# The experts' last 32 slots on 512-wide column tiles, with their products at other places in an expert's order

## The chip, the cores and the metric

The kernel runs on one core of one Trainium2 chip. The metric is the device time of one execution in microseconds (us). The engines of a core are TensorE (PE; its weight loads, which overlap with its products, are listed as PEld), VectorE (DVE), ScalarE (ACT), GpSimd (POOL) and SyncE (SP, which here only issues DMAs).

## What is computed

One decoder layer on 2048 tokens of 1024 values: a mixer (gated linear attention beside dilated window attention), a mixture of experts, and a norm. The change touches the mixture of experts alone. Cut to that:

```python
def hier_moe(n, w_grp, b_grp, w_exp, b_exp, w1, w3, w2):      # n: 2048 x 1024
    g_idx = argmax(x @ w_grp + b_grp)                          # one of 4 groups
    top_v, top_i = top_k(e_logits of that group, 2)            # two of its 8 experts
    gate = softmax(top_v) * g_prob
    for each expert e, for its tokens xb:                      # 32 experts
        hb = silu(xb @ w1[e]) * (xb @ w3[e])                   # 1024 -> 512
        out[tokens] += gate * (hb @ w2[e])                     # 512 -> 1024
h = h + out;  y = rmsnorm(h)
```

All is float32, and each expert's weights are 6 MB.

## The kernel before

The layer runs in stages one after the other: the mixer (to about 1100 us of the span), router and table of tokens (to about 1310 us), the experts (to about 2165 us), and the final norm. Each expert has 160 slots for tokens in the table. The first 128 are one full tile. The last 32 are computed apart, on tiles of 32 columns of the array, so that four small products run side by side in its four column groups.

**Weights.** `weights(e)` loads an expert's six parts of 1 MB in the order w1 first half, w3 first half, w1 second half, w3 second half, w2 first half, w2 second half (SP, L1283) into six `raw` buffers, and splits each: `hi` is the rounded copy (ACT, L1288), `lo` the rest (DVE, L1288). `hi` and `lo` have five buffers each. The full tile is multiplied in three products (hi.hi, lo.hi, hi.lo) of rounded values; the last 32 slots multiply the raw float32 weights directly, and the trace shows each of these matmuls as two instructions.

**One expert e**, in the order of the code (L1416 to L1433):
- `up` (L1327): 48 products 128x512 of the token tile (`nh`, `nl`) with w1 and w3 (L1338 to L1340), first half of the weights, then second. Then the last 32 slots (L1347): four column groups, two for w1 and two for w3, each with 256 of the 512 columns and `nr` as the stationary operand, in tile `r`. Then h = silu(w1 part) * w3 part (ACT L1352, DVE L1353), and the same for the last slots, 64 partitions by 256 (hr, L1358, L1359).
- `across` (L1363): h is transposed on PE (L1365) and split into `hh` (ACT) and `hl` (DVE, L1368); hr is transposed (L1373) and copied to `ht` (DVE, L1375).
- `turn` (L1310): the next expert's token tile is transposed (L1313) and split (L1316). In one expert of four (e = 1, 5, 9, ...) `turn_last` does the same for the last slots of the next four experts, which gives `nr` (L1322, L1324).
- `down` (L1378): 24 products with w2 (L1387 to L1389), scaled by the gate (L1391 ACT, L1393 DVE) and added to the output in memory by an indirect DMA from POOL (L1394). Then the last slots' products (L1402): four column groups of 256 of the 1024 columns each, all 128 partitions scaled (L1405), added by a second indirect DMA (L1406).

After the last expert, blocks of finished tokens are gathered (L1235), normalized and written (L1250, L1252).

**What sets the order.** A planner in the compiler lays down a fixed order for every engine's queue. It plays the program through with times of its own; each engine takes, of the instructions that are ready in it, the one that stands first in the code. A later one gets in front only while earlier ones wait. `self.behind(later, earlier)` makes the planner put one instruction after another on an engine. On the chip an engine works its queue off strictly in that order, with semaphores for what comes from other engines.

Of the kernel before, what the change touches and what calls it, by code (L numbers as in the profile page):

```python
# [19 lines left out]
KD = D // 128  # L20
# [36 lines left out]
class Layer:  # L57
# [1113 lines left out]
    def moe(self):  # L1171
        tc, nc, a = self.tc, self.nc, self.a
        with self.moest as st:
# [9 lines left out]
            acc4 = self.acc.rearrange("t (g c) -> (t g) c", g=4)  # L1183
# [3 lines left out]
            i4A = keep.tile([128, NE], I32, name="i4")  # L1187
# [3 lines left out]
            def entries(es):  # L1191
# [10 lines left out]
                f4 = gp.tile([128, NE], F32, name="f4", bufs=1)  # L1202
                nc.vector.tensor_copy(f4[:, es], irA[:, es, 0])
                nc.vector.tensor_scalar(f4[:, es], f4[:, es], 4.0, self.gcol, OP.mult, OP.add)
                nc.vector.tensor_copy(i4A[:, es], f4[:, es])
# [104 lines left out]
            def turn(G):  # L1310
                tp = tps.tile([128, KD, 128], F32, name="tp")
                for k in range(KD):
                    nc.tensor.transpose(tp[:, k, :], G[:, k * 128:(k + 1) * 128], self.ident)  # L1313
# [13 lines left out]
            def up(w, x, nr=None):  # L1327
# [5 lines left out]
                for half in range(2):  # L1333
                    for m in range(2):
                        raw, hi, lo = w[m][half]
                        for kk in range(4):
                            k = half * 4 + kk
                            nc.tensor.matmul(ps[m], nh[:, k, :], hi[:, kk, :], start=k == 0, stop=False)  # L1338
                            nc.tensor.matmul(ps[m], nl[:, k, :], hi[:, kk, :], start=False, stop=False)  # L1339
                            nc.tensor.matmul(ps[m], nh[:, k, :], lo[:, kk, :], start=False, stop=k == KD - 1)  # L1340
                pr = None
                if nr is not None:
                    pr = rps.tile([128, 256], F32, name="r")
                    for k in range(KD):
                        for g in range(4):
                            raw = w[g // 2][k // 4][0]
                            nc.tensor.matmul(pr[32 * g:32 * g + 32], nr[:, k, :], raw[:, k % 4, (g % 2) * 256:(g % 2) * 256 + 256],  # L1347
                                             start=k == 0, stop=k == KD - 1, skip_group_check=True, tile_position=(0, 32 * g))
                h = gp.tile([128, 512], F32, name="h")
# [4 lines left out]
                hr = None  # L1354
                if nr is not None:
                    hr = gp.tile([128, 256], F32, name="hr")
                    by, to = (lambda t: t.rearrange("t (p k) -> t k p", k=2)), hr[64:128].rearrange("t (k p) -> t k p", k=2)
                    nc.scalar.activation(to, by(pr[0:64]), AF.Silu)  # L1358
                    nc.vector.tensor_tensor(to, by(pr[64:128]), to, OP.mult)  # L1359
                return h, hr  # L1360

            def across(h, hr):
                tp = mm.tile([128, 4, 128], F32, name="mm")  # L1363
# [189 lines left out]
```

## Time and profile before

| | us |
|---|---|
| median of 3 runs (2217.42 to 2219.65) | 2219.3 |
| the profiled execution | 2223.29 |
| its span, first to last instruction | 2221.3 |
| PE busy in it | 2086.3 |
| DVE busy | 1272.1 |
| ACT busy | 1060.2 |
| POOL busy | 474.5 |

Durations are taken from the profiled execution, which has 2.0 us around its span and lies 4.0 us above the median. Matmuls are pipelined: the next one starts before the last has ended, so the cost of one in a row of many is the distance between starts, not its own duration. A row of the timeline that stands for several instructions (x46) gives the start of the first and the time to the end of the last.

### The profile page before, as it was taken

Reading aid. Unit: us, or ns where it says so; the run is one execution under the profiler, and the core shown is the slowest. Engines: PE = TensorE matmul, PEld = TensorE weight load, DVE = VectorE, ACT = ScalarE, POOL = GpSimd, SP = SyncE. Lnnn points to the kernel's source line nnn. Section 1 sums busy time; section 2 is a strip of 40 time slices with the busy share of each in tenths; the row PEclk is TensorE's granted clock in tenths of the full one; section 3 lists DMA queues with packets and bytes.
Section 4 is the critical chain, followed back from the end, with each engine's and each line's share of the span. In section 5 each row is a group of like instructions: output and inputs, shape, how many; then the busy total and the mean of one; then the engine's idle time right before and its main releaser. Section 6 shows DMA issues by size and latency. Waiting matters only on the chain. (4 is left out here: it accounts for less than half of the span.)

```text
span 2221.3 us, 38624 instructions
## 1 busy us (share of the span) xinstructions
PE 2086.3 (94%) x15306; PEld 1567.7 (71%) x15306; DVE 1272.1 (57%) x2452; ACT 1060.2 (48%) x1809; POOL 474.5 (21%) x362
## 2 busy tenths in 40 slices
PE   7999999999997999999999968899999999999990
PEld 7799889799885766666667756567676766767760
DVE  5203336424435466666656766567767677777663
ACT  5412335523323366867723334355555555555552
POOL 2000000000002012351321342523212222222235
PEclk9999999999998999999999969999999999999995
DMA  8333333333316524453368728688888888878886
GB/s 254 109 124 100 114 124 110 102 113 124 109 68 190 178 68 138 146 135 100 88 204 279 238 80 293 198 290 305 298 294 281 307 308 304 305 279 287 307 277 234
DMA packets 189033, 436.59 MB, mean 197 GB/s; under 512 B 35041, under 2 KB 106530, under 8 KB 162978
## 3 DMA queue, kind: packets, MB, share of 16 engines
q1 hardware_dynamic: 139090, 347.65, 44.5%
q0 software_dynamic: 21488, 60.36, 10.4%
q10 hardware_dynamic: 28272, 26.09, 4.0%
q8 instruction: 122, 2.00, 0.4%
q14 instruction: 61, 0.50, 0.1%
HBM read 342.48 MB, written 92.08 MB: 196 GB/s over the span
## 5 line engine op out<-in xcount | busy, mean ns | idle before, releaser
L1288 DVE TENSOR_TENSOR lo<-raw,hi 128x2048 fp32r<-128x2048 f32 x192 | 438.8, 2289 | 121.8 <-ACT hi L1288 121.4
L1288 ACT CAST hi<-raw 128x2048 fp32r<-128x2048 f32 x192 | 365.1, 1906 | 198.5 <-DMA raw<-expert_w 181.0
L564 ACT ACTIVATE P<-P,st 128x256 f32<-128x256 f32 (+1 forms) x384 | 173.9, 455 | 96.8 <-DVE st L562 92.5
L213 PE MATMUL mm<-whi,nh 128*128 128x256 f32 x768 | 219.9, 286 | 0.0
L215 PE MATMUL mm<-whi,nl 128*128 128x256 f32 x768 | 218.1, 284 | 0.0
L214 PE MATMUL mm<-wlo,nh 128*128 128x256 f32 x768 | 217.7, 284 | 0.0
L1340 PE MATMUL mm<-lo,nh 128*128 128x512 f32 x512 | 207.3, 406 | 0.1
L1338 PE MATMUL mm<-hi,nh 128*128 128x512 f32 x512 | 204.6, 400 | 1.1 <-ACT nh L1316 1.1
L1339 PE MATMUL mm<-hi,nl 128*128 128x512 f32 x512 | 201.4, 393 | 0.0
L128 POOL TENSOR_TENSOR ss<-ss,mhalf 128x1 f32<-128x1 f32 (+3 forms) x40 | 34.6, 865 | 699.1 <-DVE ss L127 698.9
L562 DVE CUSTOM_DVE_ANT_0 P<-s,amask 128x256 f32<-128x256 f32 (+1 forms) x384 | 124.9, 362 | 66.2 <-PE s L558 42.6
L190 PE MATMUL mm<-nh,whi 128*128 128x512 f32 x384 | 154.5, 402 | 0.0
L191 PE MATMUL mm<-nl,whi 128*128 128x512 f32 x384 | 153.1, 399 | 0.0
L192 PE MATMUL mm<-nh,wlo 128*128 128x512 f32 x384 | 152.7, 398 | 0.0
L213 PEld LDWEIGHTS mm<-whi,nh 128*128 128x128 f32 x768 | 145.4, 189 | 2.0 <-issue 0.7
L214 PEld LDWEIGHTS mm<-wlo,nh 128*128 128x128 f32 x768 | 145.7, 190 | 0.8 <-DVE wlo L176 0.4
L215 PEld LDWEIGHTS mm<-whi,nl 128*128 128x128 f32 x768 | 144.9, 189 | 0.1
L1347 PE MATMUL r<-raw,nr 128*32 128x256 f32 x2048 | 143.0, 383 | 0.0
L1394 POOL DMA_INDIRECT acc<-y,it x32 | 93.9, 2934 | 228.7 <-ACT y L1391 222.5
L558 PE MATMUL s<-k,q 64*128 64x256 f32 (+1 forms) x768 | 132.8, 416 | 0.3 <-DVE st L562 0.3
L1340 PEld LDWEIGHTS mm<-lo,nh 128*128 128x128 f32 x512 | 96.7, 189 | 43.1 <-issue 19.4
L176 DVE TENSOR_TENSOR wlo<-raw,whi 128x1024 fp32r<-128x1024 f32 x48 | 57.0, 1221 | 112.7 <-ACT whi L175 112.7
(340 smaller groups left out, 4165.0 us busy)
## 6 DMA issues: line engine op xcount, KB each, us to landing
raw<-expert_w SPq DMA_DIRECT2D x192, 1024.0 KB
raw<-w_in ACTq DMA_DIRECT2D x48, 512.0 KB
fb<-fac SPq DMA_DIRECT2D x24, 384.0 KB
x<-x SPq DMA_DIRECT2D x16, 512.0 KB
og<-og SPq DMA_DIRECT2D x32, 256.0 KB
xr<-x SPq DMA_DIRECT2D x32, 256.0 KB
v<-av SPq DMA_DIRECT2D x8, 1024.0 KB
hp<-xr SPq DMA_DIRECT2D x32, 256.0 KB
```

The lines of the kernel that those rows point to most:

```text
L190: nc.tensor.matmul(ps, hi[:, k, ms], nh[q][:, k, :], start=k == 0, stop=False)
L191: nc.tensor.matmul(ps, hi[:, k, ms], nl[q][:, k, :], start=False, stop=False)
L192: nc.tensor.matmul(ps, lo[:, k, ms], nh[q][:, k, :], start=False, stop=k == KD - 1)
L213: nc.tensor.matmul(ps[:, j, :], h, hi[:, k, :], start=j == 0 and k == 0, stop=False, skip_group_check=True)
L214: nc.tensor.matmul(ps[:, j, :], h, lo[:, k, :], start=False, stop=False, skip_group_check=True)
L215: nc.tensor.matmul(ps[:, j, :], l, hi[:, k, :], start=False, stop=k == KD - 1, skip_group_check=True)
L564: nc.scalar.activation(P[:, h, 0:w], P[:, h, 0:w], AF.Exp, bias=nm, scale=-1.0, accum_out=dn)
L1288: split = nc.scalar.copy(hi, raw), nc.vector.tensor_tensor(lo, raw, hi.bitcast(F32), OP.subtract)
L1338: nc.tensor.matmul(ps[m], nh[:, k, :], hi[:, kk, :], start=k == 0, stop=False)
L1339: nc.tensor.matmul(ps[m], nl[:, k, :], hi[:, kk, :], start=False, stop=False)
L1340: nc.tensor.matmul(ps[m], nh[:, k, :], lo[:, kk, :], start=False, stop=k == KD - 1)
L1347: nc.tensor.matmul(pr[32 * g:32 * g + 32], nr[:, k, :], raw[:, k % 4, (g % 2) * 256:(g % 2) * 256 + 256], start=k == 0, stop=k == KD - 1, ...
```

## The change

The last 32 slots' products move and get twice the width; each becomes half as many instructions.
- `up_last` is new and is called ahead of `up`, except in expert 0. Its four column groups take two steps of the contraction at once: w1 and w3 for an even k, w1 and w3 for the odd one, 512 columns each. The two partial sums are added behind it (ACT copy, DVE add), then Silu, then two multiplies. `up`'s wide products are put behind `up_last`'s of the same half of the weights.
- `down_last` (with `across_last`, the transposes of hr) is new and is called ahead of `across`. Its four column groups are two steps of the contraction by two halves of 512 columns; ACT scales one half of the partitions, DVE scales the other and adds. The indirect add goes out in 64 rows of 512 values where it was 128 rows of 256. h's transposes are put behind its last product, and the next tile's transposes behind h's.
- h, hh, hl, hr and ht have one buffer each where it was two.
- Expert 0 turns expert 1's tile before `across`.

```diff
-            def turn(G):
+            def turn(G, after=None):
                 tp = tps.tile([128, KD, 128], F32, name="tp")
                 for k in range(KD):
...
+                    t = nc.tensor.transpose(tp[:, k, :], G[:, k * 128:(k + 1) * 128], self.ident)
+                    if after is not None:
+                        self.behind(t, after, "these cover the copies of the inner values")
                 nh = gp.tile([128, KD, 128], F32R, name="nh")
                 nl = gp.tile([128, KD, 128], F32R, name="nl")
                 self.turned = nc.scalar.copy(nh, tp), nc.vector.tensor_tensor(nl, tp, nh.bitcast(F32), OP.subtract)
...
                 nc.vector.tensor_copy(nr[:, :, 0:n], tp[:, :, 0:n])
                 return nr
-            def up(w, x, nr=None):
+            def up_last(w, nr):
+                pr = rps.tile([128, 512], F32, name="r")
+                halves = []
+                for k in range(0, KD, 2):
+                    for g in range(4):
+                        kk, raw = k + g // 2, w[g % 2][k // 4][0]
+                        lasts = nc.tensor.matmul(pr[32 * g:32 * g + 32], nr[:, kk, :], raw[:, kk % 4, :],
+                                                 start=k == 0, stop=k == KD - 2, skip_group_check=True, tile_position=(0, 32 * g))
+                    halves.append(lasts)
+                hr = gp.tile([128, 256], F32, name="hr", bufs=1)
+                sm = gp.tile([64, 512], F32, name="sm", bufs=1)
+                sg = gp.tile([64, 512], F32, name="sg", bufs=1)
+                nc.scalar.copy(sm, pr[64:128])
+                nc.vector.tensor_tensor(sm, pr[0:64], sm, OP.add)
+                nc.scalar.activation(sg[32:64], sm[0:32], AF.Silu)
+                by = lambda t, u: t[:, 256 * u:256 * u + 256].rearrange("t (p k) -> t k p", k=2)
+                for u in range(2):
+                    to = hr[64 + 32 * u:96 + 32 * u].rearrange("t (k p) -> t k p", k=2)
+                    nc.vector.tensor_tensor(to, by(sm[32:64], u), by(sg[32:64], u), OP.mult)
+                return hr, halves[1::2]
+            def up(w, x, halves=None):
                 nh, nl = x
                 ps = []
                 for m in range(2):
...
                         raw, hi, lo = w[m][half]
                         for kk in range(4):
                             k = half * 4 + kk
...
+                            first = nc.tensor.matmul(ps[m], nh[:, k, :], hi[:, kk, :], start=k == 0, stop=False)
+                            if halves and kk == 0:
+                                self.behind(first, halves[half], "the raw weights come free early")
                             nc.tensor.matmul(ps[m], nl[:, k, :], hi[:, kk, :], start=False, stop=False)
                             nc.tensor.matmul(ps[m], nh[:, k, :], lo[:, kk, :], start=False, stop=k == KD - 1)
...
+                h = gp.tile([128, 512], F32, name="h", bufs=1)
                 by, to = (lambda t: t.rearrange("t (a p k) -> t a k p", a=2, k=2)), (lambda t: t.rearrange("t (a k p) -> t a k p", a=2, k=2))
                 nc.scalar.activation(to(h), by(ps[0]), AF.Silu)
                 nc.vector.tensor_tensor(to(h), by(ps[1]), to(h), OP.mult)
...
-            def across(h, hr):
+                return h
+            def across(h, after=None):
                 tp = mm.tile([128, 4, 128], F32, name="mm")
                 for k in range(4):
...
+                    self.inner = nc.tensor.transpose(tp[:, k, :], h[:, k * 128:(k + 1) * 128], self.ident)
+                    if after is not None:
+                        self.behind(self.inner, after, "the last slots' products cover the inner values")
+                hh = gp.tile([128, 4, 128], F32R, name="hh", bufs=1)
+                hl = gp.tile([128, 4, 128], F32R, name="hl", bufs=1)
                 self.crossed = nc.scalar.copy(hh, tp), nc.vector.tensor_tensor(hl, tp, hh.bitcast(F32), OP.subtract)
...
-            def down(w2, x, it, irs, e=None):
...
+                return hh, hl
+            def across_last(hr):
+                tr = rps.tile([128, 2, 64], F32, name="r")
+                for c in range(2):
+                    nc.tensor.transpose(tr[:, c, :], hr[64:128, c * 128:(c + 1) * 128], self.ident[64:128, 64:128])
+                ht = gp.tile([128, 2, 2, 32], F32, name="ht", bufs=1)
+                nc.vector.tensor_copy(ht, tr.rearrange("p c (u s) -> p u c s", u=2))
+                return ht
+            def down_last(w2, hr, ir, i2, e):
+                ht = across_last(hr)
+                pr = rps.tile([128, 512], F32, name="r")
+                for k in range(0, 4, 2):
+                    raw = w2[k // 2][0]
+                    for g in range(4):
+                        kk, f = g // 2, g % 2
+                        last = nc.tensor.matmul(pr[32 * g:32 * g + 32], ht[:, k // 2, kk, :], raw[:, kk, f * 512:f * 512 + 512],
+                                                start=k == 0, stop=k == 2, skip_group_check=True, tile_position=(0, 32 * g))
+                yr = yp.tile([64, 512], F32, name="yr", bufs=2)
+                nc.scalar.activation(yr, pr[64:128], AF.Copy, scale=ir[64:128, 1:2].bitcast(F32))
+                nc.vector.scalar_tensor_tensor(yr, pr[0:64], ir[0:64, 1:2].bitcast(F32), yr, op0=OP.mult, op1=OP.add)
+                added(nc.gpsimd.indirect_dma_start(out=acc2, out_offset=bass.IndirectOffsetOnAxis(ap=i2, axis=0),
+                                                   in_=yr, in_offset=None, compute_op=OP.add), e)
+                return last
+            def down(w2, x, it, e=None):
+                hh, hl = x
                 y = yp.tile([128, D], F32, name="y", bufs=2)
                 gate = it[:, 1:2].bitcast(F32)
                 for f in range(2):
...
                         nc.vector.tensor_scalar(y[:, fs], py, gate, None, OP.mult)
                 added(nc.gpsimd.indirect_dma_start(out=self.acc, out_offset=bass.IndirectOffsetOnAxis(ap=it[:, 0:1], axis=0),
                                                    in_=y, in_offset=None, compute_op=OP.add), e)
...
-                h = across(*up((w1, w3), x, nr[:, :, at:at + 32]))
+                if e == 0:
+                    h = up((w1, w3), x)
+                hr, halves = up_last((w1, w3), nr[:, :, at:at + 32])
+                if e:
+                    h = up((w1, w3), x, halves)
                 at += 32
+                if e == 0:
+                    x = turn(G.pop(1))
+                    self.firstst.close()
+                    yp = pool("e_y", 1)
+                h = across(h, down_last(w2, hr, irA[:, e], i2A[:, e:e + 1], e))
                 if e + 1 < NE:
-                    x = turn(G.pop(e + 1))
+                    if e:
+                        x = turn(G.pop(e + 1), self.inner)
                     if e % 4 == 1:
                         nr, at = turn_last(R, 32 * min(4, NE - 1 - e)), 0
-                    for t, c in zip(self.turned, self.crossed):
+                    for t, c in zip(self.turned, self.crossed if e else ()):
                         self.behind(t, c, "what the tensor engine waits for comes first")
-                if e == 0:
-                    self.firstst.close()
-                    yp = pool("e_y", 1)
-                down(w2, h, itA[:, e], (irA[:, e], i4A[:, e:e + 1]), e)
+                down(w2, h, itA[:, e], e)
```

Left out of the diff: the index arithmetic (`i2 = 2 * token + group` for 64 partitions in place of `i4 = 4 * token + group` for 128) and the removed old lines of `up`, `across` and `down`, which the kernel above shows.

## Rows read from the trace of the kernel before

**Rows 1.** The page, busy time (share of the span) and instructions of each engine

```profile
PE 2086.3 (94%) x15306; PEld 1567.7 (71%) x15306; DVE 1272.1 (57%) x2452; ACT 1060.2 (48%) x1809; POOL 474.5 (21%) x362
```

**Rows 2.** Busy time by stretch: length, engines, granted clock, DMA share, GB/s

```profile
1420.60:1501.30 80.70, 79.69 (x557) 54.07 (x555) 57.60 (x46) 42.82 (x33) 21.87 (x10) 1.00 0.80 275
...
1603.60:1705.80 102.20, 102.20 (x737) 71.57 (x736) 71.92 (x54) 58.38 (x44) 24.08 (x13) 1.00 0.85 296
```

**Rows 3.** Waits, 1501 to 2155 us, SP and ACT: total, times, longest

```profile
SPq L1283 <- PE r L1347: 361.6, 46, 17.3
...
ACT hi L1288 <- DMA raw<-expert_w: 158.2, 140, 3.4
```

**Rows 4.** Order of time on PE, one expert: start, length, line, shapes, count

```profile
1653.80 0.50 PE L1338 MATMUL mm<-hi,nh 128*128 128x512 f32 x1
...
1657.20 1.05 PE L1347 MATMUL r<-raw,nr 128*32 128x256 f32 x10
1658.18 0.50 PE L1340 MATMUL mm<-lo,nh 128*128 128x512 f32 x1
...
1663.89 0.64 PE L1347 MATMUL r<-raw,nr 128*32 128x256 f32 x8
...
1666.96 2.79 PE L1347 MATMUL r<-raw,nr 128*32 128x256 f32 x46
1669.68 0.66 PE L1365 MATMUL mm<-ident,h 128*128 128x128 f32 x4
...
1671.14 0.33 PE L1373 MATMUL r<-ident,hr 64*128 64x64 f32 x2
1671.40 0.73 PE L1387 MATMUL mm<-hi,hh 128*128 128x512 f32 x2
...
1677.17 1.93 PE L1402 MATMUL r<-raw,ht 128*32 128x256 f32 x32
1679.04 0.50 PE L1338 MATMUL mm<-hi,nh 128*128 128x512 f32 x1
```

**Rows 5.** The same view, another expert

```profile
1615.96 3.22 PE L1347 MATMUL r<-raw,nr 128*32 128x256 f32 x54
```

**Rows 6.** Groups by line and shape: busy us, mean ns of one, idle before

```profile
L1347 PE MATMUL r<-raw,nr 128*32 128x256 f32 x1664 | 115.2, 383 | 0.0
...
L1353 DVE TENSOR_TENSOR h<-mm,h 128x512 f32<-128x512 f32 x26 | 18.0, 692 | 50.6 <-PE mm L1340 50.6
...
L1405 DVE TENSOR_SCALAR yr<-r,ir 128x256 f32<-128x256 f32 x25 | 11.9, 478 | 0.0
L1359 DVE TENSOR_TENSOR hr<-r,hr 64x256 f32<-64x256 f32 x26 | 11.1, 427 | 9.4 <-ACT hr L1358 9.1
...
L655 PE MATMUL mm<-f,ident 32*64 32x384 f32 x64 | 12.3, 495 | 0.0
```

**Rows 7.** Order of time on PE, an early expert, with the idle time before

```profile
1373.01 0.33 PE L1373 MATMUL r<-ident,hr 64*128 64x64 f32 x2
1373.78 1.93 PE L1402 MATMUL r<-raw,ht 128*32 128x256 f32 x30 [0.43 <-ACT hh L1368]
```

**Rows 8.** Order of time on DVE behind the wide products of rows 4

```profile
1667.13 0.69 DVE L1353 TENSOR_TENSOR h<-mm,h 128x512 f32<-128x512 f32 x1 [2.23 <-PE mm L1340]
1667.74 2.28 DVE L1288 TENSOR_TENSOR lo<-raw,hi 128x2048 fp32r<-128x2048 f32 x1
```

**Rows 9.** Order of time on PE where an early expert's `down` starts

```profile
1468.82 0.40 PE L1402 MATMUL r<-raw,ht 128*32 128x256 f32 x1
1468.83 0.41 PE L1347 MATMUL r<-raw,nr 128*32 128x256 f32 x2
```

**Rows 10.** Order of time on POOL after the last expert

```profile
2173.09 1.61 POOL L1394 DMA_INDIRECT acc<-y,it  x1 [0.31 <-issue]
...
2182.79 1.59 POOL L1406 DMA_INDIRECT acc<-yr,i  x1 [0.30 <-issue]
...
2187.84 2.02 POOL L1235 DMA_INDIRECT raw<-acc,places  x1 [0.19 <-issue]
```

More of the change, by code (lines that the diff above doesn't have):

```diff
@@ L1182, in moe @@
             rps = pool("e_rps", 2, space=PSUM)
-            acc4 = self.acc.rearrange("t (g c) -> (t g) c", g=4)
+            acc2 = self.acc.rearrange("t (g c) -> (t g) c", g=2)
             table = self.table.rearrange("(e r) c -> r e c", e=NE)
@@ L1186, in moe @@
             irA = keep.tile([128, NE, 2], I32, name="ir")
-            i4A = keep.tile([128, NE], I32, name="i4")
+            i2A = keep.tile([64, NE], I32, name="i2")
             irG = keep.tile([128, NE // 4, 2], I32, name="irg")
@@ L1201, in entries @@
                                           reason="the whole table is read")
[L1202 to L1205, printed above, removed]
+                f2 = gp.tile([64, NE], F32, name="f2", bufs=1)
+                nc.vector.tensor_copy(f2[:, es], irA[0:64, es, 0])
+                nc.vector.tensor_scalar(f2[:, es], f2[:, es], 2.0, self.gcol[0:64], OP.mult, OP.add)
+                nc.vector.tensor_copy(i2A[:, es], f2[:, es])
             places = keep.tile([128, NT], I32, name="places")
@@ L1353, in up @@
                 nc.vector.tensor_tensor(to(h), by(ps[1]), to(h), OP.mult)
[L1354 to L1360, printed above, removed]
@@ L1395, in down @@
                                                    in_=y, in_offset=None, compute_op=OP.add), e)
-                if ht is not None:
-                    ir, i4 = irs
-                    pr = rps.tile([128, 256], F32, name="r")
-                    for k in range(4):
-                        raw = w2[k // 2][0]
-                        for g in range(4):
-                            nc.tensor.matmul(pr[32 * g:32 * g + 32], ht[:, k // 2, k % 2, :], raw[:, k % 2, g * 256:g * 256 + 256],
-                                             start=k == 0, stop=k == 3, skip_group_check=True, tile_position=(0, 32 * g))
-                    yr = yp.tile([128, 256], F32, name="yr", bufs=2)
-                    nc.vector.tensor_scalar(yr, pr, ir[:, 1:2].bitcast(F32), None, OP.mult)
-                    added(nc.gpsimd.indirect_dma_start(out=acc4, out_offset=bass.IndirectOffsetOnAxis(ap=i4, axis=0),
-                                                       in_=yr, in_offset=None, compute_op=OP.add), e)
             G, R = self.first
@@ L1454, in moe @@
                 x = turn(gx)
-                down(w2, across(*up((w1, w3), x)), it, None)
+                down(w2, across(up((w1, w3), x)), it)
                 m = nc.values_load(cur[:, 2:3], min_val=0, max_val=NT)
```

23 lines of the change are left out of this document (removed).

## The prediction

> **What bounds the kernel now.** I read the page's shares first: PE is busy 94% of the span, VectorE (DVE) and ScalarE (ACT) far less [rows 1]. A share over the whole span mixes stages, so the second view is the busy time by stretch. The change touches only the expert loop, and there, over four experts, PE is busy for the whole 102.2 us, while the DMA engines stand at 0.85 and DVE at 72 of 102 us; three early experts take 80.7 us [rows 2]. So one expert costs 25.55 us (102.2/4) in steady state and 26.9 us (80.7/3) early, and PE alone sets it. The waits agree: in this stretch PE's own list of waits is empty, while the weight queue sits behind the last slots' products (361.6 us) and the casts behind the weights (158.2 us) [rows 3]. The weights come as late as they may, and not too late.
>
> Third, the order of time on PE in one expert [rows 4], from 1653.80 to 1679.04, 25.24 us. To be seen there: the 48 wide products of `up` are cut into pieces of 14, 24 and 10 by the last slots' products (L1347, x10, x8, x46), and the first piece takes 3.40 us, the second 5.71; then h's transposes and the next tile's (L1365, L1313) to 1671.14, hr's transposes 0.26, `down` 5.77, the last slots' second products (L1402) 1.87. PE has something at every moment, so what the change does to the time is what it does to PE's sequence and to the holes in it.
>
> **Part 1: 512-wide column tiles.** Instructions come in fours, one for each 32 columns of the array. Three blocks give the price of a four: 32 instructions (8 fours) take 1.87 us, 46 (11.5 fours, counted as 12) take 2.72, so (2.72 - 1.87)/4 = 0.2125 us a four and 0.17 for getting into and out of the block; 54 should take 14 x 0.2125 + 0.17 = 3.15, and the block of 54 shows 3.22 with its last end [rows 4, 5]. A four of twice the width has no row. From above, width times price: 0.425. From below, durations: 256 columns take 383 ns each and 384 columns 495 [rows 6], 112 ns for 128 columns, so 512 would last 607; if the cadence went with that ratio it would be 0.2125 x 607/383 = 0.337. I take 0.425, because 112 ns for 128 columns is 0.224 us for 256, which is the cadence itself: the columns fill it and nothing is left over for the instruction. So half as many instructions of twice the width save nothing: `up`'s last slots 16 x 0.2125 = 8 x 0.425 = 3.40 us, `down`'s 1.70.
>
> The Trainium skill (TensorEngine Tiling (Array Packing), Instruction Overhead) says that each matmul carries about 60 cycles of overhead. By it the 48 instructions that an expert loses would give back an estimated 1.2 us of PE. The rows leave no room for it in a block of fours; it is the fourth rival below.
>
> **Part 2: first products in front.** They read the raw weights, which are there before the casts, so nothing cuts the wide products any more, if the planner lays both halves down together. Wide products cost (5.71 - 3.40)/10 = 0.231 each and 0.17 a piece [rows 4]; 48 in one piece are 11.26 us. With the last slots' block of 3.40 + 0.17 this is 14.83, where rows 4 show 15.88 (1653.80 to 1669.68): **1.05 us less an expert**. Every fourth expert is cut once, not twice (the block of 54 [rows 5]), and gains 0.17 + 0.17 less and half a four: 0.65. The mean is (3 x 1.05 + 0.65)/4 = 0.95. If the halves stay apart, 0.34 goes back.
>
> A second effect: the raw buffers come free at the head of an expert, not at its end, so the weight queue's wait for L1347 [rows 3] shrinks and loads start earlier by about the length of the wide products, 11 us. I price this at zero, since PE does not wait for weights; the same slack covers the other new costs on DVE and ACT. If that cover went, each lo split is 2.28 us [rows 8].
>
> **Part 3: second products ahead of h's transposes.** Before, the block of 46 or 54 stood between the last wide product and h's transposes and hid Silu and the multiply. After, the cover is hr's transposes, the copy of ht on DVE, then L1402 (1.87 us). The products of L1402 wait for ht, and h's transposes and the next tile's are tied behind them. Where a trace of before lets L1402 follow L1373 directly, it starts 0.77 us after it, PE idle for 0.43 [rows 7]. Against the 0.26 of today that is a hole of 0.51 us with DVE free. But DVE has h's multiply (0.69 [rows 6]) ready at the same moment, and, with earlier weights, a lo split under way more often: now DVE idles 2.23 us before that multiply because no weights are there yet [rows 8]. The hole is thus 0.5 at least, 0.5 + 0.69 + 2.28 = 3.5 at most. I take 1.5, near the case with the multiply ahead and little left of a split.
>
> The hole can be filled: the next expert's first products need only raw weights, nr and a free bank. The planner has done this in early experts, where L1347 of the next expert stands among L1402 of this one [rows 9]. Filled, the hole costs one more piece, 0.17 to 0.34, say 0.25. In every fourth expert nr of the next group isn't made yet, and it stays open. Mean: 0.75 x 0.25 + 0.25 x 1.5 = **0.56 us more**.
>
> **The small parts.** ACT gains a copy of 64x512, a Silu of 32x512 and the scaling of 64x512 for the old Silu of 64x256; by DVE's rows of like size each lies between 0.43 (L1359) and 0.69 us (L1353), so ACT has some 1.3 us more. DVE: an add of 64x512 (0.69), two multiplies of up to 0.43 for one, the output 0.69 for 0.478 (L1405) [rows 6]: some 1.35 us on 18 of 25.55 [rows 2]. Neither becomes the bound. POOL: the add of yr goes ahead of the add of y; each waits for the other's landing, as before, and behind them stands only a gather that is used an expert later: nothing. Its 64 rows of 2 KB for 128 of 1 KB move the same bytes. hh, hl and h have one buffer for two; each is read out before the next is written: nothing. Index arithmetic happens once.
>
> **The sum**, against the profiled execution of 2223.3 us. Experts 6 to 31: 26 x (0.95 - 0.56) = 10.1 us less. Experts 3 to 5 cost 26.9 where steady ones cost 25.55, in still more pieces: 1.5 each; experts 1 and 2, which stand under other waits, 0.4 each: 5.3. Expert 0 keeps its wide products first and gets the chain through ht in front of h's transposes: +1 (0 to 0.77 + 1.87 = 2.6 [rows 4, 7]). End: the last add before the final gathers is yr's at 2182.79, with y's at 2173.09 and the gather at 2187.84 [rows 10]. After, y's is last: between 9.7 us earlier and 5 later (one landing more, 2187.84 - 2182.79); I take 3 earlier. Total -10.1 - 5.3 + 1 - 3 = **-17.4**: 2205.9 in the profiled execution. That one lies 4.0 us above the median of 2219.3, so the forecast for the median is **2202**.
>
> **The rivals.**
> - *The hole stays open.* If the planner doesn't take the next expert's products there, or DVE on the chip comes later than planned, each of 31 experts pays 1.5: 31 x (1.5 - 0.95) = 17 more, with the end's -3 and expert 0's +1 about **2234**. It decides from a mean hole of about 1.1 us. For it: DVE's 2.28 us splits can't be broken off, and the chain h, ht, L1402, L1365 is serial. Against: rows 9, and that in the steady stretch the chip followed the planned order without one wait on PE.
> - *The pieces stay.* If the two halves of the first products go down apart, 0.34 comes back: 26 x (0.95 - 0.34 - 0.56) = 1, plus 2 early, 3 at the end and expert 0: about **2214**.
> - *The weight stream takes over.* 0.85 of 25.55 is 21.7 us of DMA an expert, against 24 to 25 of PE after. It doesn't bind, unless loads that start together land later: then nothing is won, **2219**.
> - *Instructions cost by themselves.* With 0.337 for a wide four, 12 fours save 1.06 us an expert more, 33 us in all: **2169**. Rows 6 speak against it. The rule of the Trainium skill (TensorEngine Tiling (Array Packing), Instruction Overhead) would point this way.
>
> **How the numbers follow.** Forecast 0.55 (own range 2187 to 2212: from every hole filled, 18 us for the 10, with the full 9.7 at the end, to 0.4 more in each expert), hole open 0.20, pieces stay 0.15, weight stream 0.05, instructions 0.05. A range of 8 in 10 reaches from 2178 (holes filled, early experts 1.5 each, the full 9.7 at the end: -18 - 7.5 - 9.7 = -35, and a bit of the last rival) to 2236, the open hole at its price. 0.2% (4.4 us) is about what a measurement of this kernel tells from no change. Faster: nearly all of the forecast (0.52), 0.10 of the pieces, 0.05: 0.67. Same: 0.14, from the edges and the stream. Slower: 0.19, nearly all from the open hole.
>
> **What would show it.** Fours of the new L1347 and L1402 some 0.43 us apart (0.34 would mean the last rival). One piece of 48 wide products an expert and 14.8 us for both. Between hr's transposes and the second products: next expert's first products (right), or PE idle over 1 us, waiting for ht (wrong). The weight queue waiting less for the last slots, ACT less for weights. DMA share about 0.88. If PE waits for lo, the slack that I gave for free was not there. If the first products don't fill the hole in most experts, the prediction fails with its sign.

## The result and the profile after

| | before | after |
|---|---|---|
| median of the runs beside each other, us | 2219.5 | 2310.4 |
| ratio (95% interval) | | 1.0418 (1.0402 to 1.0434) |
| span of the profiled execution, us | 2221.3 | 2307.8 |
| first wide product of the experts to that of expert 6, us | 184.7 | 198.2 |
| from there to TensorE's last product (26 experts), us | 663.3 | 751.9 |
| from there to the end of the span, us | 56.8 | 42.8 |

The change makes the kernel 4.2% slower. The forecast was 2202 with a range to 2236: the sign and the range are both wrong. Of the 86.5 us between the two spans, 88.6 came in the 26 steady experts and 13.5 in the first six; the end gave 14.0 back, and the stages ahead of the experts 1.6. The dividing line is the first wide product of expert 6. In the changed kernel that expert's first products (3.6 us) stand ahead of this line, before they stood behind it; counted by expert, the steady ones lost 92.2 and the first six 9.9.

The busy time by stretch of the changed kernel (length; PE, PEld, DVE, ACT, POOL; granted clock, DMA share, GB/s) answers to [rows 2]:

```profile
1513.00:1600.00 87.00, 80.32 (x424) 52.28 (x421) 57.75 (x46) 49.90 (x41) 16.05 (x10) 1.00 0.85 292
1600.00:1750.00 150.00, 133.14 (x701) 87.47 (x700) 101.58 (x81) 82.56 (x68) 34.93 (x18) 0.97 0.75 252
```

PE was busy for the whole of such a stretch; now it is idle for 17 us of 150, and the granted clock is no longer 1.00 throughout. The waits of PE in this stretch (1513 to 2265), a list that was empty before, say for whom:

```profile
PE r L1401 <- ACT hi L1288: 29.2, 12, 3.7
PE r L1401 <- DVE ht L1391: 21.7, 12, 2.0
PE r L1337 <- DVE nr L1326: 17.5, 6, 3.0
PE mm L1378 <- DVE h L1372: 7.0, 1, 7.0
```

Three places: the last slots' second products (L1401), some 2 us in every expert; in every fourth expert their first products (L1337), 3 us behind the copy nr; and h's transposes (L1378), once 7.0 us, in the last expert, where the multiply that makes h stands on DVE behind the norm of finished tokens (L1250), and this behind POOL:

```profile
2251.02 2.48 DVE L1250 SCALAR_TENSOR_TENSOR raw<-raw,ss,fg 128x1024 f32<-128x1024 f32 x2 [5.82 <-POOL ss L128]
2253.42 0.68 DVE L1372 TENSOR_TENSOR h<-mm,h 128x512 f32<-128x512 f32 x1
```

The first row of the waits names a cast on ACT, but a wait for several things is put down to one of them; the order of time on PE and on DVE in one expert shows who was last. PE, one expert (start, length, line, count, idle before), against [rows 4]:

```profile
1694.75 0.34 PE L1389 MATMUL r<-ident,hr 64*128 64x64 f32 x2
1697.53 1.92 PE L1401 MATMUL r<-raw,ht 128*32 128x512 f32 x16 [2.45 <-ACT hi L1288]
1699.39 0.66 PE L1378 MATMUL mm<-ident,h 128*128 128x128 f32 x4
1699.88 1.04 PE L1313 MATMUL tp<-ident,G 128*128 128x128 f32 x8
1700.85 3.63 PE L1337 MATMUL r<-raw,nr 128*32 128x512 f32 x30
1704.41 0.73 PE L1419 MATMUL mm<-hi,hh 128*128 128x512 f32 x2
1705.07 1.04 PE L1337 MATMUL r<-raw,nr 128*32 128x512 f32 x2
```

DVE over the same hole, which answers to [rows 8]:

```profile
1694.34 2.29 DVE L1288 TENSOR_TENSOR lo<-raw,hi 128x2048 fp32r<-128x2048 f32 x1
1696.55 0.69 DVE L1372 TENSOR_TENSOR h<-mm,h 128x512 f32<-128x512 f32 x1
1697.15 0.28 DVE L1391 COPY ht<-r 128x128 f32<-128x128 f32 x1
```

The hole is DVE's queue: a split that began just as the wide products ended, then h's multiply, then the copy ht (done at 1697.43), then L1401 at 1697.53. ACT's cast had ended at 1696.57 (1694.67 + 1.90), a microsecond earlier.

Grouping PE's starts gives a ledger: the time from the first start of each block to the start of the next block, summed over the blocks of experts 6 to 31. The column "steady" is the stretch from the first wide product of expert 6 to TensorE's last product. Where first products lead, expert 6's block of them lies ahead of that stretch, so a row adds up to some 4 to 5 us more than this column (in e4, where second products of expert 5 lie inside the stretch, to 3 less). "hr" is the transposes of the last slots' inner values with whatever idle time stands behind them, "nr" the transposes of gathered rows likewise. The first row is the kernel before, the second the changed one, and the others are the runs below.

| | steady | wide up | first products | second products | wide down | hr | h | next tile | nr |
|---|---|---|---|---|---|---|---|---|---|
| before | 663 | 300.2 | 110.2 | 51.4 | 151.2 | 7.1 | 13.6 | 23.7 | 5.8 |
| after | 752 | 290.5 | 118.7 | 60.9 | 156.5 | 64.5 | 15.8 | 25.3 | 23.4 |
| e1_hr_early | 688 | 292.8 | 118.3 | 50.1 | 161.5 | 6.9 | 15.5 | 23.4 | 23.3 |
| e2_own_bank | 681 | 286.7 | 105.1 | 55.4 | 165.1 | 7.0 | 15.4 | 27.9 | 23.3 |
| e7_split_held | 718 | 288.6 | 119.3 | 49.9 | 165.4 | 37.4 | 14.9 | 24.3 | 23.3 |
| e8_nr_only | 760 | 302.1 | 120.8 | 66.1 | 160.2 | 67.3 | 16.9 | 26.5 | 4.6 |
| e10_order_only | 756 | 288.9 | 122.5 | 57.9 | 157.8 | 68.0 | 17.0 | 24.1 | 23.3 |
| e3_first_in_front | 712 | 307.7 | 113.4 | 48.7 | 158.6 | 32.2 | 16.1 | 34.4 | 4.6 |
| e4_width_only | 790 | 299.1 | 95.7 | 47.5 | 234.9 | 7.1 | 49.7 | 47.8 | 5.3 |
| e4b_second_in_time | 741 | 291.4 | 112.8 | 54.6 | 164.5 | 14.2 | 32.9 | 57.4 | 13.1 |
| e5_early_nr | 654 | 292.1 | 115.5 | 47.9 | 152.4 | 6.9 | 15.5 | 24.1 | 4.6 |
| e11_narrow_one_piece | 646 | 291.2 | 102.8 | 52.6 | 153.0 | 6.8 | 14.6 | 24.2 | 4.9 |
| e9_one_piece | 637 | 291.3 | 92.2 | 47.9 | 159.1 | 6.7 | 15.5 | 22.9 | 5.4 |

Before against after: the hole behind hr's transposes 57.4, nr 17.6, second products 9.5, first products 8.5, the wide products of `down` 5.3, the rest small; the wide products of `up` gave 9.7 back.

The third and fourth terms hold the granted clock. In five steady experts the second products behind a hole took 2.5 to 3.6 us instead of 1.85, 5.6 more in all, and behind four of the waits for nr the first products took 4.85 to 5.27 instead of 3.57, 6.2 more in all. The rest of the third term is the last expert's wait for h (7.0), less the pieces in which the second products stood before (3.3). Two of the lowered stretches, and one that was not:

```profile
1697.53:1699.39 1.86, 1.86 (x17) 0.47 (x17) 1.86 (x1) 0.00 (x0) 0.00 (x0) 1.00 0.01 4
1737.90:1742.75 4.85, 4.85 (x32) 1.12 (x32) 2.14 (x1) 0.00 (x0) 3.63 (x1) 0.73 0.59 132
...
1812.89:1816.07 3.18, 3.18 (x16) 0.65 (x16) 2.10 (x1) 0.00 (x0) 0.00 (x0) 0.57 0.07 13
```

The clock granted in the second and third stretch was 0.73 and 0.57, between its two levels (1.2 and 2.4 GHz, that is 0.5 and 1.0); PE had stood idle for 2.95 and 2.44 us just before. In the first it was 1.00, behind 2.45 us.

### The profile page after: what moved, and what is told of

Its sections match the earlier page's. It is cut to its first block, busy times and chain, and to the rows that moved or that the text cites. A ratio compares the mean times of both kernels' runs of the same rounds, so it can differ in the third digit from the quotient of the medians.

```text
span 2307.8 us, 35702 instructions
## 1 busy us (share of the span) xinstructions
PE 2090.4 (91%) x13770; PEld 1525.8 (66%) x13770; DVE 1311.3 (57%) x2516; ACT 1105.1 (48%) x1873; POOL 478.8 (21%) x362
## 5 line engine op out<-in xcount | busy, mean ns | idle before, releaser
L1367 PE MATMUL mm<-lo,nh 128*128 128x512 f32 x512 | 199.9, 390 | 0.0
L1337 PE MATMUL r<-raw,nr 128*32 128x512 f32 x1024 | 151.1, 630 | 25.5 <-DVE nr L1326 23.5
L1426 POOL DMA_INDIRECT acc<-y,it x32 | 99.3, 3104 | 235.3 <-ACT y L1423 224.8
L1401 PE MATMUL r<-raw,ht 128*32 128x512 f32 x512 | 72.3, 687 | 70.0 <-ACT hi L1288 36.1
```

Of the source, the lines that this page charges most:

```text
L1337: lasts = nc.tensor.matmul(pr[32 * g:32 * g + 32], nr[:, kk, :], raw[:, kk % 4, :], start=k == 0, stop=k == KD - 2, skip_group_check=True, ...
```

## The experiments

The theory, from these traces: ht comes late because its copy stands behind a split and h's multiply on DVE, and the next expert's first products can't fill the hole, because there are two PSUM buffers `r`, claimed in the order of the code: hr's transposes, second products, next first products. The third claim needs the first one's buffer back, and that is read out by the copy ht, the very thing that the hole waits for. The rival causes: the width, with the copy, sum and multiplies that it adds to ACT and DVE; the wait for nr; the places of the blocks. Runs of the kernel before on the same chip stand beside each run: 2226.6 for the runs e1, e2, e3 and e4, 2217.8 for the others. What a run loses or wins is taken against these; the changed kernel lost 90.9.

**e1_hr_early.** hr's transposes and ht are called right behind the first products, an expert's wide products ahead of their use.

```diff
                 hr, halves = up_last((w1, w3), nr[:, :, at:at + 32])
+                ht = across_last(hr)
...
-            def down_last(w2, hr, ir, i2, e):
-                ht = across_last(hr)
+            def down_last(w2, ht, ir, i2, e):
```

> The changed kernel, with hr's transposes and the copy of ht issued right behind the first products, ahead of the wide ones, so that ht is there long before the second products. Hole theory (the loss sits between hr's transposes and the second products, where PE waits for ht behind DVE's splits and the multiply of h): in the 26 steady experts the 64.5 us from hr's transposes to the second products fall to under 15, the second products' 60.8 us (some of them at half clock after the wait) to about 50, and the median from 2310 to 2225 to 2245; the wait for nr in every fourth expert stays (17 us). Rival, width theory (512-wide tiles or the added ACT and DVE work cost the time by themselves): within 1% of 2310.

Measured: 2246.9, ratio 1.0097 (1.0071 to 1.0123), 20.3 lost in place of 90.9; just above what was expected. The hole is gone: hr falls from 64.5 to 6.9, the second products from 60.9 to 50.1. Three experts in four start 24.9 to 25.0 us apart, as fast as before. Every fourth takes 29.8 to 31.7 (26.8 before), and PE's waits (1513 to 2200) show why:

```profile
PE r L1337 <- DVE nr L1326: 17.4, 6, 3.0
PE mm L1419 <- DVE hl L1383: 10.1, 7, 1.8
```

In that expert the next first products have no nr yet. So PE waits 3 us for it, runs them at a lowered clock, and before that lacks them as cover for the copies of h: the wide products of `down` wait for hl.

**e2_own_bank.** Everything of the changed kernel, but hr's transposes and the second products get a PSUM buffer of their own, so that the first products never stand in line behind them.

```diff
-            rps = pool("e_rps", 2, space=PSUM)
+            rps = pool("e_rps", 1, space=PSUM)
+            r2s = pool("e_r2s", 1, space=PSUM)
...
-                tr = rps.tile([128, 2, 64], F32, name="r")
+                tr = r2s.tile([128, 2, 64], F32, name="s")
...
-                pr = rps.tile([128, 512], F32, name="r")
+                pr = r2s.tile([128, 512], F32, name="s")
```

> The changed kernel, with the two PSUM banks that the last slots share in turn divided: one for the first products' sums alone, the other for hr's transposes and the second products' sums. Nothing else moves by hand. Bank theory (the next expert's first products could not fill the hole, because the bank they come to in turn is claimed only after the second products have theirs): the planner now puts the next expert's first products between hr's transposes and the second products in most experts, PE's wait there shrinks from 2 us to a few tenths, and the median falls to 2235 to 2260, with the wait for nr left. Rival (the fill is kept out by weights or nr that come late, or ht comes later on the chip than planned in any case): the wait stays at 2 us and the median above 2290.

Measured: 2241.9, ratio 1.0073 (1.0051 to 1.0094), 15.4 lost, as the theory had it. In every second expert the next one's first products now stand in the hole, as the prediction had assumed (PE, one expert):

```profile
1678.77 0.34 PE L1390 MATMUL s<-ident,hr 64*128 64x64 f32 x2
1679.04 3.64 PE L1338 MATMUL r<-raw,nr 128*32 128x512 f32 x32
1682.49 1.90 PE L1402 MATMUL s<-raw,ht 128*32 128x512 f32 x16
```

In the experts between, hr's transposes stand close behind the first products, ahead of the wide ones, much as in e1. hr is 7.0, and the first products, where they stand whole in the hole, take 3.46. It was the shared buffers that kept the hole open: their number is the same, only the claims on them are divided. The wait for nr stays here too (23.3).

**e7_split_held.** The changed kernel, with one split of the next expert, that of its second part (w3, first half), held behind ht.

```diff
-                nc.vector.tensor_copy(ht, tr.rearrange("p c (u s) -> p u c s", u=2))
+                self.moved = nc.vector.tensor_copy(ht, tr.rearrange("p c (u s) -> p u c s", u=2))
...
-                w1, w3, w2 = weights(e, held.get(e, lambda: {})())
+                w1, w3, w2 = weights(e, held[e]() if e in held else {1: [(1, self.moved)]})
```

> The changed kernel with one wait more: VectorE's low-part split of the first part of the next expert's weights is held behind the copy ht of the last slots' transposed inner values, so that no split of 2.3 us can stand between the last wide product and ht. Theory (the hole in front of the second products is the multiply for the 128 slots and ht, stretched by a split that lies in between on VectorE): the hole falls from about 2.3 to about 1.2 us in the experts that had a split there, 1 us in each of 26 steady experts, and the second products with it get back to 1.85 us where they ran at half the clock: 25 to 35 us less than the changed kernel, about 2275 to 2285. Rival (the length of the hole is set by the bank alone, or by ScalarE): within 8 us of the changed kernel's 2310. Both leave the wait for nr in every fourth expert where it is.

Measured: 2274.9, ratio 1.0261 (1.0241 to 1.0281), 57.2 lost in place of 90.9. The hole without a split, on PE and on DVE:

```profile
1706.28 0.33 PE L1389 MATMUL r<-ident,hr 64*128 64x64 f32 x2
1707.39 1.92 PE L1401 MATMUL r<-raw,ht 128*32 128x512 f32 x16 [0.79 <-DVE ht L1391]
...
1706.45 0.69 DVE L1372 TENSOR_TENSOR h<-mm,h 128x512 f32<-128x512 f32 x1 [1.46 <-PE mm L1367]
1707.06 0.28 DVE L1391 COPY ht<-r 128x128 f32<-128x128 f32 x1
```

Multiply and copy alone leave 0.8 us; the split had added 1.2 to 1.7. And behind these holes the second products take 1.85 in all 25 experts (49.9 for 60.9). The last expert is apart: its hole is 8.2 us, behind the norm of finished tokens on DVE, and makes 8.5 of the 37.4.

**e8_nr_only.** The changed kernel, with the gathered rows turned one expert earlier into a second buffer.

```diff
-                nr = gp.tile([128, KD, 128], F32, name="nr", bufs=1)
+                nr = gp.tile([128, KD, 128], F32, name="nr", bufs=2)
...
+                    if e % 4 == 0 and e + 2 < NE:
+                        soonnr = turn_last(R, 32 * min(4, NE - 2 - e))
                     if e % 4 == 1:
-                        nr, at = turn_last(R, 32 * min(4, NE - 1 - e)), 0
+                        nr, at = soonnr, 0
```

> The changed kernel with the gathered rows of the last slots turned one expert earlier into a second buffer nr, nothing else. The trace of the changed kernel has 17 us more in front of and in those turns (the first products that follow wait for the copy nr, behind a split on VectorE, in every fourth expert) and the 32 first products behind them take 4.86 instead of 3.57 us. Theory (a wait of the path): 15 to 25 us less than 2310, about 2285 to 2295. Rival (the wait overlaps the hole in front of the second products, which grows by as much): within 8 us of 2310.

Measured: 2315.3, ratio 1.0439 (1.0418 to 1.0459): no gain, as the rival had it, though not by its mechanism alone. The wait itself is gone (nr 23.4 to 4.6), but the hole and the second products lost 8.0 of it again, and `up` with what stands behind it 11.6, almost all in the last three experts. There PE waited 10.7 us for hr in the last expert. DVE's queue has the norm of finished tokens (L1250) in front of hr, and this waited for POOL, which had gathers, writes and an add to issue first:

```profile
2252.39 2.48 DVE L1250 SCALAR_TENSOR_TENSOR raw<-raw,ss,fg 128x1024 f32<-128x1024 f32 x2 [7.33 <-POOL ss L128]
2254.90 0.85 DVE L1349 TENSOR_TENSOR hr<-sm,sg 32x256 f32<-32x256 f32 x2
```

**e5_early_nr.** Both: e1's edit and e8's.

> The kernel with the last slots' transposes right behind their first products, as already run (2246.9), and with the gathered rows turned one expert earlier into a second buffer nr. That kernel's ordinary experts start 24.9 to 25.0 us apart and every fourth 31.1 to 31.7, where the kernel before has 24.9 to 25.2 and 26.8. Theory (hole and nr wait are the whole of what the changed kernel lost among the steady experts): every fourth expert comes down to about 27, so 6 to 7 times 4 to 5 us less, some 30, and the end's gain of about 14 us stays: 2205 to 2222, even with the kernel before or a little faster. Rival (the early experts and the longer chain through ScalarE and VectorE hold it back): 2235 or more.

Measured: 2197.5, ratio 0.991 (0.9884 to 0.9936), faster than the kernel before and better than expected. It stands 20.3 below the kernel before; of what the changed one lost, that is 111.1 won, where e1's edit alone gave 70.6 and e8's alone nothing: an edit that takes away one of two waits in the same loop needn't show its worth by itself. Every fourth expert now takes 25.8.

**e9_one_piece.** e5, and from expert 3 on h's transposes are put behind all of the next expert's first products.

```diff
+                if e > 2:
+                    self.behind(self.inner0, halves[1], "the next first products in one piece")
```

> As the run with both waits taken away (transposes of the last slots' inner values early, nr one expert early), and the transposes of the 128 slots' inner values behind all of the next expert's first products, so that these stay in one piece and cover the copies' chain. Theory (what is left over the sum of the products is pieces that hand over between fours and wide products, and copies that TensorE waits for): 10 to 25 us below that run, 2185 to 2205, below the kernel before. Rival (the delay of the 128 slots' transposes makes hh and hl late for the wide second products): a wait of the wide second products for hl of 1 us or more in an expert, and a time above that run by 10 to 30 us.

Measured: **2177.1**, ratio 0.9822 (0.9802 to 0.9842), the fastest of all, and below the range that was expected. The order of time on PE in one expert:

```profile
2004.22 0.33 PE L1391 MATMUL r<-ident,hr 64*128 64x64 f32 x2
...
2014.00 1.92 PE L1402 MATMUL r<-raw,ht 128*32 128x512 f32 x16
2015.74 3.62 PE L1337 MATMUL r<-raw,nr 128*32 128x512 f32 x32
2019.29 0.66 PE L1378 MATMUL mm<-ident,h 128*128 128x128 f32 x4
2019.78 1.04 PE L1313 MATMUL tp<-ident,G 128*128 128x128 f32 x8
```

No bracket with idle time is left up to the last expert, the blocks are whole, and the first products cost 92.2 in place of 110.2. The stretch is busy throughout at full clock, with DMA at 0.87, where it stood at 0.85 [rows 2]:

```profile
1600.00:1702.00 102.00, 101.99 (x587) 67.22 (x588) 82.21 (x65) 66.24 (x54) 23.60 (x13) 1.00 0.87 306
```

**e10_order_only.** The changed order with the old column tiles: 256 columns, `up_last` and `down_last` with the products, the Silu, the multiply and the scatter of the kernel before; h, hh, hl, hr and ht keep the one buffer of the change.

```diff
-                pr = rps.tile([128, 512], F32, name="r")
+                pr = rps.tile([128, 256], F32, name="r")
...
+                nc.scalar.activation(to, by(pr[0:64]), AF.Silu)
+                nc.vector.tensor_tensor(to, by(pr[64:128]), to, OP.mult)
```

> The changed order of the work on the column tiles of the kernel before, 256 wide: 64 first products and 16 second products in an expert, one Silu and one multiply for the last slots, sums scattered in quarters of a row. Theory (the loss is made by the order: the second products wait for ht, whose copy stands behind VectorE's multiply and a split): a hole of 2 to 2.5 us per expert as in the changed kernel, 2290 to 2330. Rival (the hole comes with the width, by the copy, the sum and the two multiplies that it adds on ScalarE and VectorE): 2230 or less.

Measured: 2316.7, ratio 1.0449 (1.0428 to 1.047). The whole loss is there without the width, and so is the hole:

```profile
1721.07 0.34 PE L1383 MATMUL r<-ident,hr 64*128 64x64 f32 x2
1723.48 1.93 PE L1394 MATMUL r<-raw,ht 128*32 128x256 f32 x32 [2.08 <-ACT hi L1288]
```

**e11_narrow_one_piece.** e9 with these narrow column tiles.

> The run that is faster than both kernels (transposes of the last slots early, nr one expert early, first products in one piece; 2177), with the column tiles 256 wide as in the kernel before. Theory (a four costs by its columns: 0.21 us at 256 and 0.43 us at 512, so that the width alone saves no time on TensorE, and what was won is the order's): 2172 to 2190. Rival (fewer and wider instructions are worth the 1.0 us per expert that the products of the last slots take less there than before): 2200 to 2215.

Measured: 2185.6, ratio 0.9857 (0.9839 to 0.9875). The width is worth 8.5 us in the best order (2185.6 against 2177.1), and 8.0 in the changed one (98.9 lost against 90.9): a small gain, in place of none. Each run is taken here against its own runs of before; the distance of ordinary experts, 24.5 us here and 24.1 in e9, says the same. By the Trainium skill (TensorEngine Tiling (Array Packing), Instruction Overhead), which the prediction had weighed, the width would give an estimated 1.2 us in each of 32 experts, 38. The runs show less than a quarter of that.

**e3_first_in_front.** Wide tiles and first products in front, but h's transposes, hr's and the second products at their places of before (the second products called behind `down`).

```diff
-                h = across(h, down_last(w2, hr, irA[:, e], i2A[:, e:e + 1], e))
+                h = across(h)
+                ht = across_last(hr)
...
                 down(w2, h, itA[:, e], e)
+                down_last(w2, ht, irA[:, e], i2A[:, e:e + 1], e)
```

> Only the wide tiles and the first products in front; hr's transposes, second products and the next tile's transposes at the places of the kernel before (second products after down). By the prediction's second part: 48 wide products in one piece, 0.95 us less an expert, 2195. Hole theory adds: without a block of first products behind the wide ones, h's transposes are covered by 1.2 us of other transposes alone, and PE waits 0 to 1.7 us for h's multiply behind a split: 2205 to 2235. Width theory: above 2250.

Measured: 2278.2, ratio 1.0254 (1.022 to 1.0288), 51.6 lost; a miss, far above the hole theory's range, where only the width theory (above 2250) had put it. The trace puts it down to waits. The nr wait does not arise, but h's transposes have lost the block of first products that stood between them and the wide products. PE's waits, 1510 to 2230:

```profile
PE mm L1378 <- DVE h L1372: 31.0, 26, 2.5
...
PE r L1389 <- DVE hr L1349: 21.4, 2, 19.4
```

1.2 us in every expert for h, and once 19.4, in the last one, behind DVE's norm of finished tokens as in e8: together 52.4. So one half of the change without the other is a loss too. How much of it the old width would have spared at these places was not run.

**e4_width_only.** Wide tiles (with the change's single buffers of h, hh, hl, hr and ht), every product at its place of before: e3's edit and

```diff
-                hr, halves = up_last((w1, w3), nr[:, :, at:at + 32])
-                if e:
-                    h = up((w1, w3), x, halves)
+                h = up((w1, w3), x)
+                hr, halves = up_last((w1, w3), nr[:, :, at:at + 32])
```

> Only the wide tiles with their sums and half the instructions; all products at the places of the kernel before. Prediction's first part (a four of twice the width costs twice, ACT and DVE have room): 2219 within 8 us, fours 0.43 us apart. Width theory: most of the 91 us, above 2280. Instructions cost by themselves: 2190 or less.

Measured: 2352.1, ratio 1.0567 (1.0545 to 1.059), 125.6 lost; the worst miss, on the width theory's side (above 2280). The prediction had called ACT's and DVE's additional work free. The trace shows the second products among the next expert's wide products, so that the raw second weights stay held. How it came to this is a reading that no run isolates: at the old places hr comes last in the chain, the added copy, sum and second multiply make ht late, and the planner lets the next expert's wide products go first. SP's and PE's waits, 1512 to 2302:

```profile
SPq L1283 <- PE r L1400: 528.2, 49, 23.2
...
PE mm L1418 <- ACT hh L1383: 59.0, 26, 5.0
PE mm L1419 <- DVE hl L1383: 33.5, 26, 1.6
```

The weight queue waited 194 us for the second products before, and now 528; `down` waits 92.5 us for hh and hl. So the two halves of the change don't add up: the width alone loses 125.6, the order alone (e10) 98.9, both 90.9.

**e4b_second_in_time.** e4, with the next expert's wide products behind the last second product.

```diff
-                            if halves and kk == 0:
+                            if halves is not None and k == 0:
-                                self.behind(first, halves[half], "the raw weights come free early")
+                                self.behind(first, halves, "the second products come first")
...
-                h = up((w1, w3), x)
+                h = up((w1, w3), x, second if e else None)
```

> The kernel with the 512-wide column tiles alone (all products at their places in the kernel before, 2352), and in it the next expert's wide products held behind the last second product. Theory for the 130 us which the width alone lost (the two partial sums make the inner values late, the second products slide into the next expert's wide products, so that the raw second weights stay held and casts and copies come late): with the second products kept in time the raw weights come free and most of it comes back, 2230 to 2270. Rival (ScalarE's and VectorE's additional work in the chain is what costs, wherever the second products stand): above 2330.

Measured: 2292.3, ratio 1.0315 (1.0275 to 1.0354), 74.6 lost, between both theories. So 51 of the 125.6 us come back as the weights are held for less (308.1 for 528.2 in the same row) and `down` falls to 164.5. Of the remainder, PE waited 38.7 us for ht and 21.9 for h at the moved blocks. Which part of this is the added work's and which the new place's stays open.

## Why the prediction was wrong

- **What bounds the kernel**: right. PE alone set an expert's time, and each microsecond of hole went into the result.
- **Part 1, the fours**: right to the row. 32 wide instructions take 3.55 us (2015.74 to 2019.29 above), 0.42 a four after 0.17 for the piece. The width does a little better than nothing, 8 us over the kernel.
- **Part 2, one piece**: right for the wide products, 290.5/26 = 11.2 an expert for 11.26 forecast. The first products did not stay whole: in three experts of four two of 32 stand inside `down`, and such a rest costs another 0.98 us (1705.07 to 1706.05). So of the 24.7 us forecast for 26 experts, 1.2 came (410.4 to 409.2). (The 0.65 of the fourth experts comes to 0.60 by its own terms, which changes the mean by 0.01.) Where the block is whole the forecast gain appears: `up` and the first products cost 410.4 before and 383.5 in e9, 1.03 less an expert, for 0.95 forecast.
- **Part 3, the hole**: the place and the cause were named, and so was the range of 0.5 to 3.5. The value taken, 1.5, was too low: 57.4/26 = 2.2, because "little left of a split" was wrong. In every steady expert but the last a split of 2.29 reached into the hole, where DVE had idled before. The prediction had named earlier weights as the way to this and priced them at zero in part 2; e7, which holds one split back, loses 57.2 in place of 90.9.
- **The step that failed with the sign** is "the hole can be filled". Raw weights and nr were there, but "a free bank" was not: both buffers `r` are spoken for until ht is copied. [rows 9] showed next first products among second products, that is, behind ht, and never between hr's transposes and the second products, where the hole is. e2 shows that a buffer that these two don't claim was all that was missing.
- **Not priced**: in every fourth expert nr, which was said to leave the hole open, became a wait of its own in front of the first products (17.6 us), since these moved ahead of the wide products that used to hide its copy. Nor was the clock: behind some holes the products ran slower, 5.6 us in the second and 6.2 in the first products. Nor was the last expert, where the norm of finished tokens on DVE made PE wait 7.0 us for h.
- **The small parts**: free on PE's path in the changed order, as e10 shows. They were far from free at the old places (e4).
- **The end** was forecast at 3 and gave 14.0: the last add goes out 4.7 us after PE's last product, not 18.2 (POOL; [rows 10] has before's, at 2182.79 with PE's last at 2164.58):

```profile
2269.72 1.59 POOL L1426 DMA_INDIRECT acc<-y,it  x1 [0.30 <-issue]
2276.79 0.99 POOL L1235 DMA_INDIRECT raw<-acc,places  x1 [5.49 <-issue]
```

- **The early experts**: 4.3 less forecast, 9.9 more measured by expert; they have the same holes.
- **The rival** "the hole stays open" had the mechanism, at a chance of 0.20, and 2234 for its price. That was the hole at 1.5 and nothing else. A hole of 2.2 adds 18 us in the steady experts, part 2's missing gain 23.5, nr 17.6, and the second products with the last expert's wait 9.5; these are most of the way to 2310. The terms that hang on an open hole should have been added to it, and its chance should have been set by asking which buffer each filler takes, and when.

## What to carry to other kernels

Moving work ahead on the bounding engine moves a wait to whatever covered the copies of the moved step. List for each block who covered whom, and count for every filler not only its data but the buffer that it must claim, in the order of the program. When two waits sit in one loop, take both away before judging either: here one edit gave 71 us, the other nothing, and both together 111. And, as e4 suggests, a cheap chain on a second engine stays cheap only while nothing holds a weight buffer behind it.

## What the runs showed of the hardware

After idle stretches of 2.0 to 3.7 us, TensorE's granted clock fell towards its lower level for the next microseconds in some cases, not in all: second products behind holes of 2.44 us took 3.18 us in one expert (0.57 granted) and 1.85 in another (1.00, 1697.53 above). In e10, behind 23 holes of 2.08 us alike, 18 blocks of second products took 1.86 us and five 3.36 to 3.42 (0.53 to 0.54 granted). Behind the 25 holes of 0.8 to 1.2 us in the steady experts of e7 it never fell. In the changed kernel a hole cost up to 1.7 us more than its length (3.57 for 1.85), and the price of a wait can't be read from its length alone.
